# Attention with a bias on one core: transposes of later pairs issued into a PSUM buffer's gap, evacuations queued ahead of newer products

## The chip, the cores and the metric

One Trainium2 chip, of which the kernel uses one core. The metric is device time in microseconds; the number compared is the median of several executions. Beside it stands one profiled execution, from which all rows below come.

## The reference

Four batches of eight heads, 1024 positions, head dimension 64, and one bias matrix that all heads share:

```python
def reference(q, k, v, bias):            # q, k, v: [4, 8, 1024, 64]; bias: [1, 1, 1024, 1024]
    scale = 1.0 / np.sqrt(head_dim)
    scores = scale * np.matmul(q, k.transpose(0, 1, 3, 2))
    scores = scores + bias
    scores_max = np.max(scores, axis=-1, keepdims=True)
    attn = np.exp(scores - scores_max) / (np.sum(np.exp(scores - scores_max), axis=-1, keepdims=True) + 1e-8)
    return np.matmul(attn, v).astype(np.float32)
```

## The kernel before

The kernel uses exp(s + bias) = exp(s) * exp(bias): `eb` holds exp(bias) transposed, made once, and every tile of exp(scores) is multiplied by it. A column of ones in `vall` gives the row sums with the last product, so the division is done on the small output.

The 32 heads are worked in 16 pairs. A pair's K and Q are loaded (`load_qk`, GpSimd's queue, three buffers), transposed on TensorE into the PSUM tile `px` (16 transposes for K, 16 for Q) and copied out by VectorE into `kT` and `qT` (the latter times `mask`, so that each head meets only its own rows).

The unit of work is a block of 128 keys by 512 queries of one head: 512 blocks, 32 for a pair, named `banks` in the code. They run through a chain of four engines' steps:

- TensorE: three blocks of scores (`s_slot`, a "slot", into one of two PSUM buffers `ps` of three banks).
- ScalarE: one exp over the whole slot, 128x1536, into `E` (twelve buffers of two slots).
- VectorE: `mul_pair`, the product with `eb`, two blocks at a time.
- TensorE again: `av_bank` (below: AV), four matmuls of a block's `E` against `vall`, summed over eight key chunks in the PSUM tile `po`. After the eighth, VectorE evacuates `po`: a reciprocal `rs` and a multiplication into `oall` (below: the evacuation). Two query halves make an output, which SyncE's queue writes.

[...] The other two are the buffers named `xa` and `xb`: `po` of a pair's head 0 uses `xa`, of head 1 `xb`, and `px` uses the same two, Q's in `xa`, K's in `xb`. So a transpose must wait until the sum that was in its buffer is evacuated, and the next sum must wait until the transpose is copied out.

The order of everything is written out by hand under `tc.manual_schedule()`: each engine gets its instructions in the order in which the loop over `order` issues them. One step of the loop issues a slot of scores (or one of six pieces of the bias, early on), then up to three products, then three or four blocks of AV (`quota`), and behind a block of AV with `kc == 7` its evacuation. AV takes the eight blocks of head 0 first, then those of head 1 (`av_order`). The list `pend_t` says at which count of AV blocks a later pair is transposed; its check stands inside the AV loop:

```python
while t_next < len(pend_t) and pend_t[t_next][2] <= av_next and av_next % 8 == 0:
    pr, which, _ = pend_t[t_next]
    transpose(pr, which)
```

The count is a multiple of eight, so a transpose is issued right behind the block that completed a sum, and behind that sum's evacuation on VectorE. Pairs 2 to 15 are transposed in this way, 28 transposes of 16 matmuls; pairs 0 and 1 are transposed in the first steps.

Of the kernel before, what the change touches and what calls it, by code (L numbers as in the profile page):

```python
# [9 lines left out]
BF = mybir.dt.bfloat16  # L10
ACTF = mybir.ActivationFunctionType
ALU = mybir.AluOpType
# [3 lines left out]
def kernel(  # L16
# [15 lines left out]
    nc = tc.nc  # L32
    B, H, S, D = q.shape
    P = 128
    NCH = S // P
    D1 = D + 1
    NP = B * H // 2
# [12 lines left out]
    kvp = ctx.enter_context(tc.tile_pool(name="kvp", bufs=3))  # L50
    ep = ctx.enter_context(tc.tile_pool(name="ep", bufs=12))
    op = ctx.enter_context(tc.tile_pool(name="op", bufs=2))
    small = ctx.enter_context(tc.tile_pool(name="small", bufs=4))
    ps_s = ctx.enter_context(tc.tile_pool(name="ps_s", bufs=2, space=bass.MemoryType.PSUM))
    ps_x = ctx.enter_context(tc.tile_pool(name="ps_x", bufs=1, space=bass.MemoryType.PSUM))
# [5 lines left out]
    mask = consts.tile([P, 2, S], BF)  # L61
# [3 lines left out]
    trs = {}  # L65

    def load_qk(pr):
        qr = raw.tile([P, 2, NCH, D], BF, name="qr")
        kr = raw.tile([P, 2, NCH, D], BF, name="kr")
        nc.gpsimd.dma_start(out=kr.rearrange("p t c d -> p t (c d)"), in_=kf[pr])  # L70
        nc.gpsimd.dma_start(out=qr.rearrange("p t c d -> p t (c d)"), in_=qf[pr])  # L71
        raws[pr] = (qr, kr)

    def load_v(pr):
        for t in range(2):
            nc.gpsimd.dma_start(out=vall[:, 2 * pr + t, :, :D], in_=vf[pr, :, t])  # L76

    def transpose(pr, which):
        src = raws[pr][which]
        px = ps_x.tile([P, NCH, P], BF, tag="xa" if which == 0 else "xb", name="px")  # L80
        for c in range(NCH):
            for t in range(2):
                nc.tensor.transpose(px[t * D:(t + 1) * D, c, :], src[:, t, c, :], ident[:])  # L83
        if which == 0:

            dst = kvp.tile([P, 2, NCH * P], BF, name="qT")
            nc.vector.tensor_tensor(dst[:], px.rearrange("p c q -> p (c q)").unsqueeze(1).to_broadcast([P, 2, NCH * P]),  # L87
                                    mask[:], op=ALU.mult)
        else:
            dst = kvp.tile([P, NCH, P], BF, name="kT")  # L90
            nc.vector.tensor_copy(dst[:], px[:])  # L91
        trs[(pr, which)] = dst


    banks = [(pr, h, qh, kc) for pr in range(NP) for qh in range(2) for kc in range(NCH) for h in range(2)]
    NB = len(banks)
# [4 lines left out]
    def s_slot(g):  # L101
        ps = ps_s.tile([P, 3, HQ], F32, tag="s", name="ps")
        sl = slots[g]
        for j, (pr, h, qh, kc) in enumerate(sl):
            qT, kT = trs[(pr, 0)], trs[(pr, 1)]
            nc.tensor.matmul(ps[:, j, :], kT[:, kc, :], qT[:, h, qh * HQ:(qh + 1) * HQ],  # L106
                             start=True, stop=True)
        if g % 2 == 0:
            etiles[g // 2] = ep.tile([P, 6, HQ], BF, name="E")
        e = etiles[g // 2]  # L110
        o = 3 * (g % 2)
        n = len(sl)
        nc.scalar.activation(e[:, o:o + n, :], ps[:, :n, :], ACTF.Exp, scale=scale)  # L113

    def b_slot(qh, kcs):
        ps = ps_s.tile([P, 3, 2 * HQ], BF, tag="s", name="pb")
        for j, kc in enumerate(kcs):
            for i in range(QC):
                nc.tensor.transpose(ps[:, j, i * P:(i + 1) * P],  # L119
                                    btraw[:, qh * QC + i, :].rearrange("p (kp kc) -> p kc kp", kc=NCH)[:, kc, :],  # L120
                                    ident[:])
        n = len(kcs)
        nc.scalar.activation(eb[:, qh, kcs[0]:kcs[0] + n, :], ps[:, :n, :HQ], ACTF.Exp)  # L123

    def mul_pair(b):
        pr, h, qh, kc = banks[b]
        e = etiles[b // 6]
        o = b % 6
        nc.vector.tensor_tensor(e[:, o:o + 2, :], e[:, o:o + 2, :],  # L129
                                eb[:, qh, kc, :].unsqueeze(1).to_broadcast([P, 2, HQ]),  # L130
                                op=ALU.mult)
# [4 lines left out]
    def av_bank(b):  # L136
        pr, h, qh, kc = banks[b]
        if kc == 0:
            po[h] = ps_x.tile([P, QC, D1], F32, tag="xa" if h == 0 else "xb", name="po")
        acc = po[h]  # L140
        e = etiles[b // 6]
        for i in range(QC):
            nc.tensor.matmul(acc[:, i, :], e[:, b % 6, i * P:(i + 1) * P], vall[:, 2 * pr + h, kc, :],  # L143
                             start=(kc == 0 and i == 0), stop=(kc == NCH - 1), skip_group_check=True)
        if kc == NCH - 1:
            if qh == 0:
                oalls[h] = op.tile([P, NCH, D], F32, tag=f"o{h}", name="oall")
            oall = oalls[h]
            rs = small.tile([P, QC, 1], F32, name="rs")
            nc.vector.reciprocal(rs[:], acc[:, :, D:D1])  # L150
            nc.vector.tensor_tensor(oall[:, qh * QC:(qh + 1) * QC, :], acc[:, :, :D],  # L151
                                    rs[:].to_broadcast([P, QC, D]), op=ALU.mult)
            if qh == 1:
                nc.sync.dma_start(out=of[2 * pr + h], in_=oall[:])


    av_order = []
# [3 lines left out]
    with tc.manual_schedule():  # L161

        nc.vector.memset(warm[:], 0.0)
        nc.scalar.activation(warm[:], warm[:], ACTF.Exp)  # L164
        make_identity(nc, ident[:])
        load_qk(0)
        nc.gpsimd.dma_start(out=btraw[:, :QC, :], in_=bf_[:, :QC, :])
        nc.vector.memset(vall[:, :, :, D:D1], 1.0)
        for t in range(2):
            for u in range(2):  # L170
                nc.vector.memset(mask[t * D:(t + 1) * D, u, :], 1.0 if t == u else 0.0)  # L171
        load_v(0)
        load_qk(1)
        nc.gpsimd.dma_start(out=btraw[:, QC:, :], in_=bf_[:, QC:, :])
        load_v(1)
        load_qk(2)
        transpose(0, 1)
        transpose(0, 0)

        order = [("S", g) for g in range(NS)]  # L180
        halves = [(0, 1, 2), (3, 4, 5), (6, 7)]
        for at, x in ((3, (0, halves[0])), (5, (0, halves[1])), (7, (0, halves[2])),
                      (9, (1, halves[0])), (11, (1, halves[1])), (13, (1, halves[2]))):
            order.insert(at, ("B",) + x)

        done_b = -1
        mul_next = 0
        eb_have = set()
        av_next = 0
        muls_at = {}  # L190
        pend_t = [(1, 1, 4), (1, 0, 5)]
        for pr in range(2, NP):
            pend_t += [(pr, 0, (pr - 2) * 32 + 8), (pr, 1, (pr - 2) * 32 + 16)]
        t_next = 0
        loaded = 2
        for step, item in enumerate(order):
            if item[0] == "S":
                g = item[1]
                s_slot(g)
                exp_b = min(NB, 3 * (g + 1))  # L200
            else:
                b_slot(item[1], item[2])
                for kc in item[2]:
                    eb_have.add((item[1], kc))
                exp_b = done_b + 1

            n = 0
            while mul_next + 2 <= exp_b and n < 3:
                pr, h, qh, kc = banks[mul_next]
                if (qh, kc) not in eb_have:  # L210
                    break
                mul_pair(mul_next)
                muls_at[mul_next] = muls_at[mul_next + 1] = step
                mul_next += 2
                n += 1
            done_b = exp_b - 1

            quota = 4 if (exp_b - av_next) > 18 else 3
            while quota and av_next < NB:
                b = av_order[av_next]  # L220
                if muls_at.get(b, 10 ** 9) > step - 2:
                    break

                av_bank(b)
                av_next += 1
                quota -= 1
                while t_next < len(pend_t) and pend_t[t_next][2] <= av_next and av_next % 8 == 0:
                    pr, which, _ = pend_t[t_next]
                    transpose(pr, which)
                    t_next += 1  # L230
                    if which == 1:
                        if pr + 1 < NP:
                            load_qk(pr + 1)
                        if pr < NP:
                            load_v(pr)
            if step == 3:
                for _ in range(2):
                    pr, which, _ = pend_t[t_next]
                    transpose(pr, which)
                    t_next += 1  # L240

        while mul_next < NB:
            mul_pair(mul_next)
            mul_next += 2
        while av_next < NB:
            av_bank(av_order[av_next])
            av_next += 1


# [28 lines left out]
```

## Time and profile before

| what | value |
|---|---|
| median of 3 runs | 390.25 us (389.04 to 392.25) |
| profiled execution | 391.52 us, its span 389.5 us |
| mean granted TensorE clock | 0.858 |
| ScalarE, TensorE, VectorE busy | 244.1, 266.8, 234.3 us |
| HBM read, written | 29.36, 8.39 MB |

The span runs from the first to the last instruction on the core; the execution's time is 2.0 us longer. Busy times are unions of an engine's instructions. Matmuls are pipelined and their ends modelled, so TensorE's busy time is more than its work.

### The profile page before, as it was taken

Reading aid. Unit: us, or ns where it says so; the run is one execution under the profiler, and the core shown is the slowest. Engines: PE = TensorE matmul, PEld = TensorE weight load, DVE = VectorE, ACT = ScalarE, POOL = GpSimd, SP = SyncE. Lnnn points to the kernel's source line nnn. Section 1 sums busy time; section 2 is a strip of 40 time slices with the busy share of each in tenths; the row PEclk is TensorE's granted clock in tenths of the full one; section 3 lists DMA queues with packets and bytes.
Section 4 is the critical chain, followed back from the end, with each engine's and each line's share of the span. In section 5 each row is a group of like instructions: output and inputs, shape, how many; then the busy total and the mean of one; then the engine's idle time right before and its main releaser. Section 6 shows DMA issues by size and latency. Waiting matters only on the chain. (4 is left out here: it accounts for less than half of the span.)

```text
span 389.5 us, 7214 instructions
## 1 busy us (share of the span) xinstructions
PE 266.8 (69%) x3136; PEld 165.9 (43%) x3136; DVE 234.3 (60%) x422; ACT 244.1 (63%) x179; POOL 52.6 (14%) x72
## 2 busy tenths in 40 slices
PE   2756866758566697665966669476776756759894
PEld 1435434435343454433544345243443534435553
DVE  5353475865638566374566856557485473855885
ACT  1682865946558485482756749456594554947992
POOL 8340301103030030300303012030220000000000
PEclk9996799988879786697789969889696897988997
DMA  7998710808026080360803508071190010100111
GB/s 119 202 184 90 81 56 6 130 2 108 29 40 97 2 108 28 48 89 3 107 29 55 83 0 121 16 80 58 23 141 0 3 56 0 44 12 13 44 56 55
DMA packets 46911, 23.53 MB, mean 60 GB/s; under 512 B 34336, under 2 KB 42528, under 8 KB 46624
## 3 DMA queue, kind: packets, MB, share of 16 engines
q0 software_dynamic: 42272, 14.68, 34.0%
q1 hardware_dynamic: 4608, 8.39, 5.8%
q8 instruction: 24, 0.39, 0.4%
q14 instruction: 7, 0.06, 0.0%
HBM read 29.36 MB, written 8.39 MB: 97 GB/s over the span
## 5 line engine op out<-in xcount | busy, mean ns | idle before, releaser
L113 ACT ACTIVATE E<-ps 128x1536 bf16<-128x1536 f32 x171 | 235.4, 1476 | 129.1 <-PE ps L106 90.0
L129 DVE TENSOR_TENSOR E<-E,eb 128x1024 bf16<-128x1024 bf16 x256 | 169.2, 689 | 113.7 <-ACT E L113 101.5
L106 PE MATMUL ps<-qT,kT 128*128 128x512 bf16 x512 | 164.4, 437 | 17.1 <-ACT E L113 15.1
L143 PEld LDWEIGHTS <-E 128*128 128x128 bf16 x2048 | 99.6, 106 | 63.6 <-issue 22.7
L143 PE MATMUL po<-vall,E 128*128 128x65 bf16 x2048 | 110.0, 206 | 6.7 <-DVE E L129 5.1
L106 PEld LDWEIGHTS <-kT 128*128 128x128 bf16 x512 | 49.5, 108 | 56.6 <-issue 41.1
L83 PE MATMUL px<-ident,kr 128*64 128x128 bf16 x256 | 15.5, 292 | 50.2 <-DVE oall L151 44.0
L83 PE MATMUL px<-ident,qr 128*64 128x128 bf16 x256 | 13.4, 263 | 44.5 <-DVE oall L151 43.2
L70 POOL DMA_DIRECT2D kr<-in_k_dram x16 | 11.3, 708 | 226.1 <-PE px L83 219.9
L83 PEld LDWEIGHTS <-kr 128*64 128x64 bf16 x256 | 12.3, 153 | 51.7 <-issue 45.3
L83 PEld LDWEIGHTS <-qr 128*64 128x64 bf16 x256 | 10.6, 136 | 46.3 <-issue 44.5
L87 DVE TENSOR_TENSOR qT<-px,mask 128x2048 bf16<-128x2048 bf16 x16 | 19.6, 1224 | 15.4 <-PE px L83 15.4
L76 POOL DMA_DIRECT2D vall<-in_v_dram x32 | 28.1, 885 | 4.3 <-DMA btraw<-in_bias_dram 4.0
L151 DVE TENSOR_TENSOR oall<-po,rs 128x256 f32<-128x256 f32 x64 | 27.2, 424 | 2.2
L91 DVE COPY kT<-px 128x1024 bf16<-128x1024 bf16 x16 | 11.1, 691 | 17.5 <-PE px L83 17.5
L123 ACT ACTIVATE eb<-pb 128x1536 bf16<-128x1536 bf16 (+1 forms) x6 | 7.9, 1309 | 8.5 <-PE pb L119 8.5
L150 DVE RECIPROCAL rs<-po 128x4 f32<-128x4 f32 x64 | 11.3, 176 | 1.4 <-PE po L143 1.4
L71 POOL DMA_DIRECT2D qr<-in_q_dram x16 | 11.7, 728 | 0.8 <-issue 0.4
L119 PE MATMUL pb<-ident,btraw 128*128 128x128 bf16 x64 | 5.9, 252 | 0.5 <-ACT E L113 0.5
L119 PEld LDWEIGHTS <-btraw 128*128 128x128 bf16 x64 | 5.4, 151 | 1.7 <-issue 0.9
L171 DVE MEMSET mask<- 64x1024 bf16 (+1 forms) x4 | 2.8, 698 | 0.5 <-issue 0.2
L164 ACT ACT_TABLE_LOAD x1 | 1.3, 1283 | 0.7 <-PEq L262 0.7
(11 smaller groups left out, 2.6 us busy)
## 6 DMA issues: line engine op xcount, KB each, us to landing
out_dram<-oall SPq DMA_DIRECT2D x32, 256.0 KB, 2.0
kr<-in_k_dram POOLq DMA_DIRECT2D x16, 256.0 KB, 4.0
qr<-in_q_dram POOLq DMA_DIRECT2D x16, 256.0 KB, 5.4
vall<-in_v_dram POOLq DMA_DIRECT2D x32, 128.0 KB, 5.8
btraw<-in_bias_dram POOLq DMA_DIRECT2D x2, 1024.0 KB, 12.3
```

What stands on the lines that cost most here:

```text
L70: nc.gpsimd.dma_start(out=kr.rearrange("p t c d -> p t (c d)"), in_=kf[pr])
L71: nc.gpsimd.dma_start(out=qr.rearrange("p t c d -> p t (c d)"), in_=qf[pr])
L76: nc.gpsimd.dma_start(out=vall[:, 2 * pr + t, :, :D], in_=vf[pr, :, t])
L83: nc.tensor.transpose(px[t * D:(t + 1) * D, c, :], src[:, t, c, :], ident[:])
L87: nc.vector.tensor_tensor(dst[:], px.rearrange("p c q -> p (c q)").unsqueeze(1).to_broadcast([P, 2, NCH * P]), mask[:], op=ALU.mult)
L106: nc.tensor.matmul(ps[:, j, :], kT[:, kc, :], qT[:, h, qh * HQ:(qh + 1) * HQ], start=True, stop=True)
L113: nc.scalar.activation(e[:, o:o + n, :], ps[:, :n, :], ACTF.Exp, scale=scale)
L119: nc.tensor.transpose(ps[:, j, i * P:(i + 1) * P], btraw[:, qh * QC + i, :].rearrange("p (kp kc) -> p kc kp", kc=NCH)[:, kc, :], ident[:])
L129: nc.vector.tensor_tensor(e[:, o:o + 2, :], e[:, o:o + 2, :], eb[:, qh, kc, :].unsqueeze(1).to_broadcast([P, 2, HQ]), op=ALU.mult)
L143: nc.tensor.matmul(acc[:, i, :], e[:, b % 6, i * P:(i + 1) * P], vall[:, 2 * pr + h, kc, :], start=(kc == 0 and i == 0), stop=(kc == NCH - ...
L150: nc.vector.reciprocal(rs[:], acc[:, :, D:D1])
L151: nc.vector.tensor_tensor(oall[:, qh * QC:(qh + 1) * QC, :], acc[:, :, :D], rs[:].to_broadcast([P, QC, D]), op=ALU.mult)
```

## The change

The transposes and the evacuations are split from their second halves. `transpose_pe` issues the 16 matmuls and returns a function that issues VectorE's copy; `av_bank` returns a function that issues the evacuation. A step now issues, in this order: its slot of scores; a waiting transpose's matmuls, if one is due; blocks of AV; one product; the evacuations and copies that are due (`late`); up to two more products. A transpose falls due two steps behind the step in which AV reached its count (`t_wait = step + 2`), and that step issues one block of AV only (`quota = 1`). All later transposes use `xa`, and the counts are such (8 and 24 of a pair's 32) that it is head 0's sum that has just ended, so that head 1's eight blocks run in `xb` meanwhile. The products of a step are those of the slot before (`exp_b = new_b` stands at the end of the step), and a block of AV is issued three steps behind its product (`LAG`) where it was two. K and Q are asked for two pairs ahead instead of one.

```diff
--- before.py
+++ after.py
@@ -76,20 +76,27 @@
             nc.gpsimd.dma_start(out=vall[:, 2 * pr + t, :, :D], in_=vf[pr, :, t])
 
     def transpose(pr, which):
+        transpose_pe(pr, which)()
+
+    def transpose_pe(pr, which):
         src = raws[pr][which]
-        px = ps_x.tile([P, NCH, P], BF, tag="xa" if which == 0 else "xb", name="px")
+        px = ps_x.tile([P, NCH, P], BF, tag="xb" if pr < 2 and which else "xa", name="px")
         for c in range(NCH):
             for t in range(2):
                 nc.tensor.transpose(px[t * D:(t + 1) * D, c, :], src[:, t, c, :], ident[:])
-        if which == 0:
-
-            dst = kvp.tile([P, 2, NCH * P], BF, name="qT")
-            nc.vector.tensor_tensor(dst[:], px.rearrange("p c q -> p (c q)").unsqueeze(1).to_broadcast([P, 2, NCH * P]),
-                                    mask[:], op=ALU.mult)
-        else:
-            dst = kvp.tile([P, NCH, P], BF, name="kT")
-            nc.vector.tensor_copy(dst[:], px[:])
-        trs[(pr, which)] = dst
+
+        def copy():
+            if which == 0:
+
+                dst = kvp.tile([P, 2, NCH * P], BF, name="qT")
+                nc.vector.tensor_tensor(
+                    dst[:], px.rearrange("p c q -> p (c q)").unsqueeze(1).to_broadcast([P, 2, NCH * P]),
+                    mask[:], op=ALU.mult)
+            else:
+                dst = kvp.tile([P, NCH, P], BF, name="kT")
+                nc.vector.tensor_copy(dst[:], px[:])
+            trs[(pr, which)] = dst
+        return copy
 
 
     banks = [(pr, h, qh, kc) for pr in range(NP) for qh in range(2) for kc in range(NCH) for h in range(2)]
@@ -142,7 +149,10 @@
         for i in range(QC):
             nc.tensor.matmul(acc[:, i, :], e[:, b % 6, i * P:(i + 1) * P], vall[:, 2 * pr + h, kc, :],
                              start=(kc == 0 and i == 0), stop=(kc == NCH - 1), skip_group_check=True)
-        if kc == NCH - 1:
+        if kc < NCH - 1:
+            return None
+
+        def evac():
             if qh == 0:
                 oalls[h] = op.tile([P, NCH, D], F32, tag=f"o{h}", name="oall")
             oall = oalls[h]
@@ -152,6 +162,7 @@
                                     rs[:].to_broadcast([P, QC, D]), op=ALU.mult)
             if qh == 1:
                 nc.sync.dma_start(out=of[2 * pr + h], in_=oall[:])
+        return evac
 
 
     av_order = []
@@ -183,67 +194,83 @@
                       (9, (1, halves[0])), (11, (1, halves[1])), (13, (1, halves[2]))):
             order.insert(at, ("B",) + x)
 
-        done_b = -1
+        mul_done = {}
+        eb_have = set()
         mul_next = 0
-        eb_have = set()
+        exp_b = 0
         av_next = 0
-        muls_at = {}
-        pend_t = [(1, 1, 4), (1, 0, 5)]
+
+        pend_t = []
         for pr in range(2, NP):
-            pend_t += [(pr, 0, (pr - 2) * 32 + 8), (pr, 1, (pr - 2) * 32 + 16)]
-        t_next = 0
-        loaded = 2
-        for step, item in enumerate(order):
-            if item[0] == "S":
-                g = item[1]
-                s_slot(g)
-                exp_b = min(NB, 3 * (g + 1))
-            else:
-                b_slot(item[1], item[2])
-                for kc in item[2]:
-                    eb_have.add((item[1], kc))
-                exp_b = done_b + 1
-
-            n = 0
-            while mul_next + 2 <= exp_b and n < 3:
+            pend_t += [(pr, 0, (pr - 2) * 32 + 8), (pr, 1, (pr - 2) * 32 + 24)]
+        gap = None
+        LAG = 3
+
+        def muls(n):
+            nonlocal mul_next
+            while n and mul_next + 2 <= exp_b:
                 pr, h, qh, kc = banks[mul_next]
                 if (qh, kc) not in eb_have:
                     break
                 mul_pair(mul_next)
-                muls_at[mul_next] = muls_at[mul_next + 1] = step
+                mul_done[mul_next] = mul_done[mul_next + 1] = step
                 mul_next += 2
-                n += 1
-            done_b = exp_b - 1
-
+                n -= 1
+
+        t_wait = None
+        for step, item in enumerate(order):
+            prev_b = exp_b
+            if item[0] == "S":
+                g = item[1]
+                s_slot(g)
+                new_b = min(NB, 3 * (g + 1))
+            else:
+                b_slot(item[1], item[2])
+                new_b = exp_b
+            late = []
+            if step == 3:
+                transpose(1, 1)
+                transpose(1, 0)
+                load_qk(3)
             quota = 4 if (exp_b - av_next) > 18 else 3
+            if t_wait is not None and step >= t_wait:
+                pr, which, _ = pend_t.pop(0)
+                late.append(transpose_pe(pr, which))
+                t_wait = None
+                quota = 1
+                if which == 1:
+                    if pr + 2 < NP:
+                        load_qk(pr + 2)
+                    load_v(pr)
             while quota and av_next < NB:
                 b = av_order[av_next]
-                if muls_at.get(b, 10 ** 9) > step - 2:
+                if mul_done.get(b, 10 ** 9) > step - LAG:
                     break
-
-                av_bank(b)
+                e = av_bank(b)
+                if e:
+                    late.append(e)
                 av_next += 1
                 quota -= 1
-                while t_next < len(pend_t) and pend_t[t_next][2] <= av_next and av_next % 8 == 0:
-                    pr, which, _ = pend_t[t_next]
-                    transpose(pr, which)
-                    t_next += 1
-                    if which == 1:
-                        if pr + 1 < NP:
-                            load_qk(pr + 1)
-                        if pr < NP:
-                            load_v(pr)
-            if step == 3:
-                for _ in range(2):
-                    pr, which, _ = pend_t[t_next]
-                    transpose(pr, which)
-                    t_next += 1
-
-        while mul_next < NB:
-            mul_pair(mul_next)
-            mul_next += 2
+                if pend_t and av_next == pend_t[0][2]:
+                    t_wait = step + 2
+
+            muls(1)
+            for f in late:
+                f()
+            muls(2)
+            exp_b = new_b
+            if item[0] == "B":
+                for kc in item[2]:
+                    eb_have.add((item[1], kc))
+
         while av_next < NB:
-            av_bank(av_order[av_next])
+            muls(1)
+            b = av_order[av_next]
+            while mul_next <= b:
+                muls(1)
+            e = av_bank(b)
+            if e:
+                e()
             av_next += 1
 
 
```

On VectorE, around the transposes of pair 7 in the kernel before (`qT` and `kT` are the copies of a transpose; L150 and L151 are an evacuation, L129 a product):

```order
L129 TENSOR_TENSOR E_1677<-E_1677,eb_82 128x1024
L150 RECIPROCAL rs_1689<-po_1641 128x4
L151 TENSOR_TENSOR oall_1688<-po_1641,rs_1689 128x256
L87 TENSOR_TENSOR qT_1709<-px_1692,mask_83 128x2048
L129 TENSOR_TENSOR E_1677<-E_1677,eb_82 128x1024 x2
L129 TENSOR_TENSOR E_1739<-E_1739,eb_82 128x1024 x3
L150 RECIPROCAL rs_1766<-po_1711 128x4
L151 TENSOR_TENSOR oall_1765<-po_1711,rs_1766 128x256
L91 COPY kT_1786<-px_1769 128x1024
```

Each copy stands directly behind an evacuation, with no product between them, and the evacuation behind products of the slot just issued.

The same place in the changed kernel (L136 is the product, L160 and L161 the evacuation):

```order
L160 RECIPROCAL rs_1718<-po_1656 128x4
L161 TENSOR_TENSOR oall_1717<-po_1656,rs_1718 128x256
L136 TENSOR_TENSOR E_1654<-E_1654,eb_82 128x1024
L136 TENSOR_TENSOR E_1697<-E_1697,eb_82 128x1024 x2
L92 TENSOR_TENSOR qT_1768<-px_1746,mask_83 128x2048
L136 TENSOR_TENSOR E_1697<-E_1697,eb_82 128x1024
L136 TENSOR_TENSOR E_1744<-E_1744,eb_82 128x1024
L160 RECIPROCAL rs_1795<-po_1703 128x4
L161 TENSOR_TENSOR oall_1794<-po_1703,rs_1795 128x256
L136 TENSOR_TENSOR E_1744<-E_1744,eb_82 128x1024 x2
```

Three products now stand between the evacuation that frees the buffer and the copy, and one product of the copy's own step stands ahead of it.

On TensorE, the start of pair 7's K transpose in the kernel before, with the engines that a row waits for:

```order
L143 LDWEIGHTS E_1638
L143 MATMUL po_1711<-vall_84,E_1638 128x65
L83 LDWEIGHTS kr_1520 [waits DVE_49,DMASW4_49]
L83 MATMUL px_1769<-ident_79,kr_1520 64x128 [waits PE_49]
L83 LDWEIGHTS kr_1520
```

And in the changed kernel, where the sum whose buffer it takes is `po_1780`; the last block of that sum, and the start of the transpose:

```order
L150 MATMUL po_1780<-vall_84,E_1697 128x65
L150 LDWEIGHTS E_1591 [waits DVE_49]
L150 MATMUL po_1831<-vall_84,E_1591 128x65 [waits PE_49]
...
L113 MATMUL ps_1865<-qT_1495,kT_1644 128x512 [waits Activation_49]
L113 LDWEIGHTS kT_1644
...
L86 LDWEIGHTS kr_1361 [waits DVE_49,DMASW2_49]
L86 MATMUL px_1870<-ident_79,kr_1361 64x128 [waits PE_49]
```

Before, the wait for VectorE stands right behind the last AV matmul of the sum `po_1711` that must be evacuated; now two slots of scores and five blocks of AV into `po_1831` lie between.

## Rows read from the trace of the kernel before

**Rows 1.** The page's head: span, and busy time, share and instructions of each engine.

```profile
span 389.5 us, 7214 instructions
...
PE 266.8 (69%) x3136; PEld 165.9 (43%) x3136; DVE 234.3 (60%) x422; ACT 244.1 (63%) x179; POOL 52.6 (14%) x72
```

**Rows 2.** Waits over the span: who waited for whom, total us, times, longest.

```profile
POOL kr L70 <- PE px L83: 219.9, 11, 24.5
...
PE px L83 <- DVE oall L151: 87.2, 28, 3.6
...
PE po L143 <- DVE E L129: 5.1, 16, 0.8
```

**Rows 3.** Costliest groups on the page: busy us, mean ns | idle before, releaser.

```profile
L113 ACT ACTIVATE E<-ps 128x1536 bf16<-128x1536 f32 x171 | 235.4, 1476 | 129.1 <-PE ps L106 90.0
L129 DVE TENSOR_TENSOR E<-E,eb 128x1024 bf16<-128x1024 bf16 x256 | 169.2, 689 | 113.7 <-ACT E L113 101.5
...
L87 DVE TENSOR_TENSOR qT<-px,mask 128x2048 bf16<-128x2048 bf16 x16 | 19.6, 1224 | 15.4 <-PE px L83 15.4
...
L151 DVE TENSOR_TENSOR oall<-po,rs 128x256 f32<-128x256 f32 x64 | 27.2, 424 | 2.2
L91 DVE COPY kT<-px 128x1024 bf16<-128x1024 bf16 x16 | 11.1, 691 | 17.5 <-PE px L83 17.5
L123 ACT ACTIVATE eb<-pb 128x1536 bf16<-128x1536 bf16 (+1 forms) x6 | 7.9, 1309 | 8.5 <-PE pb L119 8.5
L150 DVE RECIPROCAL rs<-po 128x4 f32<-128x4 f32 x64 | 11.3, 176 | 1.4 <-PE po L143 1.4
```

**Rows 4.** Timeline around pair 7's K transpose: start us, us, engine, line, idle before.

```profile
155.30 0.99 PE L106 MATMUL ps<-qT,kT 128*128 128x512 bf16 x3
...
157.81 1.29 DVE L129 TENSOR_TENSOR E<-E,eb 128x1024 bf16<-128x1024 bf16 x2 [0.72 <-ACT E L113]
159.02 0.17 DVE L150 RECIPROCAL rs<-po 128x4 f32<-128x4 f32 x1
159.23 0.42 DVE L151 TENSOR_TENSOR oall<-po,rs 128x256 f32<-128x256 f32 x1
...
159.79 1.06 PE L83 MATMUL px<-ident,kr 128*64 128x128 bf16 x16 [3.39 <-DVE oall L151]
...
161.22 1.47 PE L106 MATMUL ps<-qT,kT 128*128 128x512 bf16 x3
...
162.78 1.45 ACT L113 ACTIVATE E<-ps 128x1536 bf16<-128x1536 f32 x1 [5.01 <-PE ps L106]
...
163.16 1.47 PE L106 MATMUL ps<-qT,kT 128*128 128x512 bf16 x3
```

**Rows 5.** Timeline of the same kernel where no transpose is near.

```profile
166.39 8.16 ACT L113 ACTIVATE E<-ps 128x1536 bf16<-128x1536 f32 x6 [0.27 <-PE ps L106]
...
166.51 0.81 PE L106 MATMUL ps<-qT,kT 128*128 128x512 bf16 x3
...
167.16 0.53 PE L143 MATMUL po<-vall,E 128*128 128x65 bf16 x12
...
167.89 0.81 PE L106 MATMUL ps<-qT,kT 128*128 128x512 bf16 x3 [0.21 <-ACT E L113]
```

**Rows 6.** Timeline of the start, pair 1's Q transpose and the first steady exp.

```profile
16.88 0.64 PE L83 MATMUL px<-ident,qr 128*64 128x128 bf16 x16 [0.64 <-DMA qr<-in_q_dram]
...
18.31 1.45 ACT L113 ACTIVATE E<-ps 128x1536 bf16<-128x1536 f32 x1 [1.92 <-PE ps L106]
...
31.06 1.47 PE L119 MATMUL pb<-ident,btraw 128*128 128x128 bf16 x12
```

**Rows 7.** Timeline, ScalarE's last exps.

```profile
353.11 29.26 ACT L113 ACTIVATE E<-ps 128x1536 bf16<-128x1536 f32 x22 [4.14 <-PE ps L106]
```

**Rows 8.** Stretches with and without transposes: us, PE, PEld, DVE, ACT, POOL busy; clock, DMA, GB/s.

```profile
150.00:166.00 16.00, 12.40 (x114) 7.66 (x115) 6.47 (x11) 7.09 (x5) 3.16 (x4) 0.61 0.25 33
...
355.00:381.00 26.00, 23.00 (x296) 13.83 (x295) 22.37 (x44) 26.00 (x20) 0.00 (x0) 1.00 0.11 42
```

## The prediction

> **What bounds the kernel now.** I read the page's head first, then the waits, then a stretch of the timeline that holds one transpose, then one that holds none. No engine is near full: ScalarE is busy 244.1 us of 389.5, VectorE 234.3, and TensorE's 266.8 is a modelled figure [rows 1]. So the time is made by engines waiting for one another in turn. The costliest exp group shows the sum of it: ScalarE sat idle 129.1 us, mostly for scores that TensorE had not made [rows 3]. The waits show why TensorE was late: 28 times a transpose (`px`) waited for an evacuation (`oall`), 87.2 us in all [rows 2]. 28 is the number of transposes of pairs 2 to 15.
>
> One of them in full [rows 4]: the scores of a slot start at 155.30. Their exp must end before VectorE makes the two products that were issued ahead of the evacuation (157.81); only then come the reciprocal (159.02) and the multiplication (159.23), and the transpose starts at 159.79, after TensorE has stood 3.39 us. Behind it in TensorE's order stand the next scores, at 161.22, so ScalarE starts at 162.78 after 5.01 us of idleness. From scores to scores that is 5.92 us. And TensorE comes back slowly: the next slot takes 1.94 us (161.22 to 163.16). [...]
>
> Without a transpose near, the kernel runs at ScalarE's pace. Six exps take 8.16 us, the first 1.45, the others 1.342 apart; TensorE's scores take 0.65 us, its three blocks of AV the rest, and it then stands 0.21 us for ScalarE [rows 5], so its work is 1.17 us of a slot of 1.34. From 355 to 381 ScalarE was busy all of 26.00 us at a granted clock of 1.00 [rows 8].
>
> **The floor that the change could reach.** ScalarE's first exp behind the start-up is at 18.31 [rows 6]; the wait ahead of it is for loads, which the change doesn't move. From there 168 slots at 1.342 are 225.5 us, and the five remaining exps of the bias are 6.4 (7.9 less the first at about 1.5) [rows 3]. The last exp ended at 382.37 and the span at 389.5 [rows 1, 7], a tail of 7.1 which stays: its last product and its last sum are in the same order. 18.3 + 225.5 + 6.4 + 7.1 = 257.3 us of span. So the 28 transposes cost (389.5 - 257.3) / 28 = 4.7 us each now. What is left of that in the changed kernel is the question.
>
> **The change part by part.**
>
> *Products one slot behind.* An evacuation no longer stands behind products that wait for the exp of the same step's slot. It waits for one product at most, and that one's exp belongs to the slot before, which is through when TensorE starts the new scores, since `ps` has two buffers. This takes the exp and a product out of the chain in [rows 4]. It costs no instruction.
>
> *Transposes two steps later.* TensorE does two slots of scores and up to seven blocks of AV between the end of a sum and the transpose into its buffer. The evacuation is queued one product (0.66 us, 169.2 over 256) behind its slot's exp and takes 0.60 (0.42 + 0.18) [rows 3]; the transpose comes about 2.1 us (1.34 + the 0.65 of the scores, and their wait) after that exp. The 3.39 us go, with some 0.8 to spare if VectorE is on time.
>
> *The transpose's own time on TensorE.* 16 matmuls took 0.64 us in an undisturbed place [rows 6] and 1.06 behind a long wait [rows 4]. I take 0.64, as nothing waits ahead of it now. The step that holds it issues one block of AV (0.17, a third of the 0.52 from 167.16 to where the wait of 0.21 began [rows 5]): 0.65 + 0.64 + 0.17 = 1.46 against 1.34, so the next scores come 0.1 late, less than TensorE's reserve. Cost 0; at 1.06 it would be 0.2 each.
>
> *The copy out, the new wait.* In the next step AV comes back to head 0, whose sum needs `xa`, and must wait for the copy. Behind that wait are queued the rest of the step's AV and then the scores that ScalarE wants. Count from the moment when the exp ahead of the copy's step ends. One product, 0.66 with its start; then `qT`, 1.22 [rows 3]: 1.9 us. Then two to four blocks of AV, 0.5, and the scores with their way to ScalarE, 0.85: 3.25. ScalarE wants them after two slots, 2.69. So it loses 0.6 us at a Q transpose if VectorE is on time. `kT` takes 0.69: 2.7 us, no loss. VectorE is not quite on time: its work per slot is (169.2 + 27.2 + 19.6 + 11.3 + 11.1) / 171 = 1.39 us [rows 3] against 1.34, though neighbouring instructions overlap a little (two products in 1.29 [rows 4]). A copy that is late by one product costs 0.6 more. I take 0.2 of lateness for Q and 0.3 for K, so 0.8 and 0.3. Bounds: nothing at all, and 1.5 for each of the 28, which is two products and an evacuation late. Each idle also starts an exp anew, 1.45 in place of 1.342, 0.1.
>
> *AV three steps behind its product.* This takes away waits that total 5.1 us on TensorE before AV [rows 2]; they were beside ScalarE's pace, so I count 0, and 5 at most as a gain. The twelve `E` buffers hold 72 blocks, and a backlog of some 24 fits.
>
> *Loads.* The issues move on GpSimd's queue: V of a pair now stands behind K and Q of two pairs on. GpSimd's 219.9 us of waits [rows 2] are for raw buffers, three of them as before; a K load waits for the transpose of the pair three earlier, as before, and V is asked for two pairs before AV needs it. 0.
>
> *Sum.* 14 x (0.8 + 0.3) + 28 x 0.1 = 18.2 us. 257.3 + 18.2 = 275.5 of span. The profiled execution lies 2.0 above its span and the median 1.3 below the profiled execution: 276.2, so **276 us**, with its bounds 257.3 + 0.7 = 258 and 257.3 + 0.7 + 28 x 1.5 = 300.
>
> [...] In the rows the granted clock is 1.00 where TensorE stops for some 0.2 us in each slot, and 0.61 around waits of 3 us [rows 8]. With the long waits gone I expect 1.00 nearly throughout. [...]
>
> **Rivals.**
>
> *VectorE is late at every copy.* The wait for an evacuation is exchanged for one for the copy, with VectorE behind by two products and an evacuation: 1.5 us at each transpose, 300 us. For it: VectorE's 1.39 us a slot, more than ScalarE's. Against: each loss of ScalarE lets VectorE catch up, and by its sum alone (238.4 from 18.8, when pair 1's copies are out, and 3 us for the last output) VectorE would be through at 260.
>
> *The wait stays where it was.* Should VectorE be two slots behind, the transpose would wait for the evacuation as now, for up to 3.1 us (87.2 / 28), but without the exp in the chain. Half of the old cost of 4.7 would be 28 x 2.35 = 66 us on the floor: 324 us. Against it: nothing holds VectorE back by so much, since its products wait only for exps that are through.
>
> [...]
>
> **How the numbers follow.** The forecast (258 to 290) gets 0.75, VectorE late at every copy (290 to 310) 0.15, the wait that stays (310 to 386) 0.06, the low clock, slower than 394, 0.02, something under 258 or within 1% of before 0.02. Eight in ten are held by 261 to 295: from nearly no loss at the copies to 1.3 us at each. A measurement of this kernel can tell about 1% from no change. Faster by more than that: 0.96; within it 0.02; slower 0.02.
>
> **What would show it.** In the changed profile, the transposes' wait for `oall` should fall from 87.2 us to under 10, and AV's wait for `qT` or `kT` should appear, some 0.6 to 1 us at a time, more at Q's than at K's. ScalarE's idle time ahead of its exps should fall from 129.1 us to under 35, its gaps one for a transpose and under 1.5 us. The granted clock should be above 0.95. VectorE should be busy 83% or more. I am wrong if the gaps of ScalarE come at other places than the transposes, if the clock falls below 0.9, or if the products (not the copies) make AV wait.

## The result

| kernel | median, us | ratio to the kernel before, 95% interval |
|---|---|---|
| before | 390.63 (4 runs, 389.04 to 392.25) | |
| changed | 266.75 (4 runs, 266.52 to 266.89) | 0.6828 [0.6799, 0.6857] |

The forecast was 276 us, in a range of 261 to 295. The profiled execution took 266.52 us, with a span of 264.5.

The page of the changed kernel, its head [rows 1] and three groups, the first two the same as in [rows 3], the third TensorE's AV:

```profile
span 264.5 us, 7204 instructions
...
PE 221.0 (84%) x3136; PEld 137.6 (52%) x3136; DVE 227.2 (86%) x422; ACT 240.7 (91%) x179; POOL 52.5 (20%) x72
...
L120 ACT ACTIVATE E<-ps 128x1536 bf16<-128x1536 f32 x171 | 232.4, 1475 | 16.7 <-PE ps L113 14.6
L136 DVE TENSOR_TENSOR E<-E,eb 128x1024 bf16<-128x1024 bf16 x256 | 167.1, 687 | 18.9 <-ACT E L120 14.1
...
L150 PE MATMUL po<-vall,E 128*128 128x65 bf16 x2048 | 94.1, 194 | 16.1 <-DVE qT L92 10.9
```

ScalarE does the same work (240.7 us against 244.1), and its idle time ahead of its exps fell from 129.1 us to 16.7. Its waits, against [rows 2]:

```profile
ACT E L120 <- PE ps L113: 14.6, 11, 9.4
...
PE po L150 <- DVE qT L92: 10.9, 14, 1.0
...
PE po L150 <- DVE kT L97: 4.3, 14, 0.4
```

No transpose waits for `oall` any more; that line of 87.2 us is gone. In its place stand the waits that the change had to bring: AV waits for a copy, 14 times for Q's (0.78 us each) and 14 times for K's (0.31). Where they reach ScalarE is seen in its timeline, which merges exps that follow one another without a gap:

```profile
18.52 1.45 ACT L120 ACTIVATE E<-ps 128x1536 bf16<-128x1536 f32 x1 [1.32 <-PE ps L113]
...
112.34 14.88 ACT L120 ACTIVATE E<-ps 128x1536 bf16<-128x1536 f32 x11 [0.48 <-ACT E L120]
127.78 13.60 ACT L120 ACTIVATE E<-ps 128x1536 bf16<-128x1536 f32 x10 [0.56 <-PE ps L113]
141.70 15.01 ACT L120 ACTIVATE E<-ps 128x1536 bf16<-128x1536 f32 x11 [0.32 <-PE ps L113]
...
231.41 26.68 ACT L120 ACTIVATE E<-ps 128x1536 bf16<-128x1536 f32 x20 [0.32 <-PE ps L113]
```

In the steady part there are 13 gaps, one per pair, of 0.32, 0.48 and 0.56 us in turn (as in the three rows from 112.34 on), 5.8 us in all. The one ahead of 127.78 in full, from the same kernel's timeline:

```profile
122.70 0.42 DVE L161 TENSOR_TENSOR oall<-po,rs 128x256 f32<-128x256 f32 x1
...
123.22 2.04 DVE L136 TENSOR_TENSOR E<-E,eb 128x1024 bf16<-128x1024 bf16 x3
123.24 0.81 PE L113 MATMUL ps<-qT,kT 128*128 128x512 bf16 x3
...
123.98 0.64 PE L86 MATMUL px<-ident,qr 128*64 128x128 bf16 x16
...
124.68 0.81 PE L113 MATMUL ps<-qT,kT 128*128 128x512 bf16 x3
...
125.17 1.22 DVE L92 TENSOR_TENSOR qT<-px,mask 128x2048 bf16<-128x2048 bf16 x1
...
126.45 0.65 PE L150 MATMUL po<-vall,E 128*128 128x65 bf16 x16 [0.95 <-DVE qT L92]
...
126.93 0.81 PE L113 MATMUL ps<-qT,kT 128*128 128x512 bf16 x3
...
127.58 0.53 PE L150 MATMUL po<-vall,E 128*128 128x65 bf16 x12
...
127.95 0.81 PE L113 MATMUL ps<-qT,kT 128*128 128x512 bf16 x3
```

The evacuation that frees the buffer ends at 123.12, and the transposes start at 123.98 without a wait. Their copy stands behind a product, the AV of head 0 behind the copy, and the scores that ScalarE wants behind AV. It is a Q transpose. No K transpose has a gap behind it.

### The profile page after: what moved, and what is told of

The parts are those of the page before. It is cut to its first block, busy times and chain, and to the rows that moved or that the text cites. A ratio compares the mean times of both kernels' runs of the same rounds, so it can differ in the third digit from the quotient of the medians.

```text
span 264.5 us, 7204 instructions
## 1 busy us (share of the span) xinstructions
PE 221.0 (84%) x3136; PEld 137.6 (52%) x3136; DVE 227.2 (86%) x422; ACT 240.7 (91%) x179; POOL 52.5 (20%) x72
## 4 chain that ended last, share of the span: by engine, by line
ACT 44%; DVE 26%; PE 18%; DMA 4%; issue 4%; POOL 2%; ACTq 0%; POOLq 0%
ACT E L120 42%; DVE E L136 16%; PE ps L113 13%; DVE qT L92 5%; PE po L150 5%; DMA qr<-in_q_dram 4%; DVE kT L97 3%; ACT eb L130 2%; DVE oall L161 2%; DVE rs L160 1%; POOL vall L76 1%; POOL kr L70 1%; ACTq L120 0%; POOL qr L71 0%; PE px L86 0%
## 5 line engine op out<-in xcount | busy, mean ns | idle before, releaser
L120 ACT ACTIVATE E<-ps 128x1536 bf16<-128x1536 f32 x171 | 232.4, 1475 | 16.7 <-PE ps L113 14.6
L136 DVE TENSOR_TENSOR E<-E,eb 128x1024 bf16<-128x1024 bf16 x256 | 167.1, 687 | 18.9 <-ACT E L120 14.1
L113 PE MATMUL ps<-qT,kT 128*128 128x512 bf16 x512 | 139.7, 382 | 14.5 <-ACT E L120 10.9
L150 PEld LDWEIGHTS <-E 128*128 128x128 bf16 x2048 | 84.2, 98 | 54.6 <-issue 19.5
L150 PE MATMUL po<-vall,E 128*128 128x65 bf16 x2048 | 94.1, 194 | 16.1 <-DVE qT L92 10.9
L113 PEld LDWEIGHTS <-kT 128*128 128x128 bf16 x512 | 44.2, 98 | 45.1 <-issue 20.7
L161 DVE TENSOR_TENSOR oall<-po,rs 128x256 f32<-128x256 f32 x64 | 27.2, 425 | 2.2
L86 PE MATMUL px<-ident,kr 128*64 128x128 bf16 x256 | 10.6, 228 | 5.8 <-DMA kr<-in_k_dram 5.8
L86 PEld LDWEIGHTS <-kr 128*64 128x64 bf16 x256 | 8.0, 113 | 11.8 <-issue 5.9
L86 PE MATMUL px<-ident,qr 128*64 128x128 bf16 x256 | 10.6, 228 | 2.0 <-DMA qr<-in_q_dram 2.0
L86 PEld LDWEIGHTS <-qr 128*64 128x64 bf16 x256 | 8.0, 113 | 8.3 <-DMA qr<-in_q_dram 5.4
L160 DVE RECIPROCAL rs<-po 128x4 f32<-128x4 f32 x64 | 11.2, 175 | 1.0 <-PE po L150 1.0
```

## The experiments

All but one start from the changed kernel; the lines that differ are shown or told, with `...` where some are left out. The theory: a transpose cost 4.7 us because an exp, products and an evacuation stood in a chain in which TensorE could do nothing else; the order on VectorE and the delay each take a part of that chain out, and what is left is the copy of Q. The rivals: the delay alone does it; or it was the low clock.

**The low clock's share.** The kernel before, with TensorE at work in its waits (26 of the 28), by matmuls whose results the next scores overwrite:

```diff
+    def fill(pr):
+        ps = ps_s.tile([P, 3, HQ], F32, tag="s", name="ps")
+        qT, kT = trs[(pr, 0)], trs[(pr, 1)]
+        for j in range(12):
+            nc.tensor.matmul(ps[:, j % 3, :], kT[:, j % NCH, :], qT[:, 0, :HQ], start=True, stop=True)
+        ready.append(ps)
...
-        ps = ps_s.tile([P, 3, HQ], F32, tag="s", name="ps")
+        ps = ready.pop() if ready else ps_s.tile([P, 3, HQ], F32, tag="s", name="ps")
...
+                    if step > 15 and order[step + 1][0] == "S":
+                        fill(slots[order[step][1]][0][0])
                     transpose(pr, which)
```

> The kernel before, with TensorE kept at work in 26 of its 28 waits: ahead of a transpose it makes 12 score matmuls into the buffer of the next slot (0.216 us each, 2.6 us in a wait of 3.1), which that slot's own scores then overwrite; they do no part of the result, and all else is the kernel before. Theory (about 2 us of the 4.7 that a transpose cost are the low clock behind the wait: 0.4 on the transposes, 0.6 on each of three slots): 26 x 2.0 = 52 us less, about 338 (325 to 350), with a granted clock above 0.97. Rival (the cost is the wait itself, and the slow slots behind it are hidden): 380 to 392 us.

It took 361.13 us, beside 389.73 for the kernel before in the same runs, a ratio of 0.9263 [0.9210, 0.9317]. The mean granted clock was 0.977, and one transpose in its timeline reads:

```profile
147.14 2.75 PE L107 MATMUL ps<-qT,kT 128*128 128x512 bf16 x12 [0.41 <-ACT E L122]
...
150.46 0.64 PE L83 MATMUL px<-ident,kr 128*64 128x128 bf16 x16 [0.57 <-DVE oall L160]
...
152.18 10.85 ACT L122 ACTIVATE E<-ps 128x1536 bf16<-128x1536 f32 x8 [3.75 <-issue]
```

28.6 us over 26 waits is 1.1 us each, not 2.0. Neither side's number held: the low clock is a real part of the old cost, but the smaller one. The 1.1 may be a little too low, since only 19 of the 28 transposes still waited for `oall`; the others came when the added matmuls had ended, which may have held them up. With a granted clock of 1.00 (145 to 165 us) ScalarE still lost 3.75 us at a transpose (5.01 in [rows 4]).

**The order on VectorE alone.** No delay: evacuation, transpose and copy are issued in the step that ends the sum.

```diff
-                    t_wait = step + 2
+                    pr, which, _ = pend_t.pop(0)
+                    muls(1)
+                    for f in late:
+                        f()
+                    late = []
+                    transpose(pr, which)
...
```

> No delay at all: in the step that ends a sum, one product, the evacuation, the transpose and its copy are issued at once, then the rest of AV; products stay one slot behind and AV three steps. Theory: the exp is out of the chain, but TensorE still stands about 1.5 us for each evacuation, its next scores come 1.9 us late, and ScalarE loses 1.7 us at each of 28 transposes: about 305 us (295 to 315), with a granted clock near 1.00, since no wait is near 3 us. So some 85 us of the gain would come from the order on VectorE and some 40 from the delay. Rival 1 (the order on VectorE is nothing, the delay all): 370 to 390 us. Rival 2 (the low clock made most of the old loss, and it is gone as soon as the waits are halved): 270 to 280 us.

318.06 us. The waits:

```profile
PE px L86 <- DVE oall L161: 47.9, 28, 1.8
```

28 waits of 1.71 us on average, a little more than the 1.5 expected. Two neighbouring transposes, the first of K, the second of Q, and the stretch around the second (us, then busy time of PE, PEld, DVE, ACT, POOL, then granted clock):

```profile
154.84 0.64 PE L86 MATMUL px<-ident,kr 128*64 128x128 bf16 x16 [1.78 <-DVE oall L161]
...
156.63 6.82 ACT L120 ACTIVATE E<-ps 128x1536 bf16<-128x1536 f32 x5 [1.87 <-PE ps L113]
...
163.53 0.70 PE L86 MATMUL px<-ident,qr 128*64 128x128 bf16 x16 [1.66 <-DVE oall L161]
...
166.16 1.45 ACT L120 ACTIVATE E<-ps 128x1536 bf16<-128x1536 f32 x1 [2.71 <-issue]
```

```profile
163.00:169.00 6.00, 5.25 (x68) 3.49 (x70) 4.02 (x7) 3.10 (x3) 0.00 (x0) 0.72 0.08 23
```

Around the first the granted clock was 1.00 (150 to 163), and ScalarE lost 1.87 us. Around the second it was 0.72 in the six microseconds around the end of the wait, and ScalarE lost 2.90 us (2.71 and, one exp later, 0.19). The page has the clock at 0.7 or 0.8 in five of its 40 slices ahead of the tail, one of them at the second transpose. If each of the five is one transpose like it, which is an estimate, they make some 5 of the 13 us above the 305 that were expected; the rest is 1.9 where 1.7 was taken, and an exp started anew each time. Rival 1 fell (without the delay, the order with all else that the change brings is worth 72 us), and rival 2 with it.

**The delay alone.** Products of the slot just issued, all else as changed: `exp_b = new_b` and the bias pieces' entry in `eb_have` move from the end of the step to ahead of its products. The evacuation still stands behind one product of its step only, where the kernel before issued up to three ahead of it.

> The products of a step are again those of the slot just issued, so every evacuation and copy stands behind a product that waits for that slot's exp; the two steps of delay, the buffers and AV's three steps are the changed kernel's. Theory: an evacuation is through 1.34 us later, which the two steps just fail to hide (0.5 us of wait), and a copy too, which nothing hides: ScalarE loses about 2.0 us at each Q and 1.5 at each K transpose, 50 us in place of 7; about 308 us (298 to 315). Rival (the two steps of delay hide it alone): 267 to 272 us.

304.86 us, ratio 0.7803 [0.7758, 0.7849]. One Q transpose:

```profile
122.14 0.64 PE L86 MATMUL px<-ident,qr 128*64 128x128 bf16 x16 [0.56 <-DVE oall L161]
...
123.44 0.69 DVE L136 TENSOR_TENSOR E<-E,eb 128x1024 bf16<-128x1024 bf16 x1 [0.24 <-ACT E L120]
...
124.05 1.22 DVE L92 TENSOR_TENSOR qT<-px,mask 128x2048 bf16<-128x2048 bf16 x1
...
125.32 0.53 PE L150 MATMUL po<-vall,E 128*128 128x65 bf16 x12 [1.54 <-DVE qT L92]
...
126.53 5.48 ACT L120 ACTIVATE E<-ps 128x1536 bf16<-128x1536 f32 x4 [1.34 <-PE ps L113]
```

Both waits that were expected are there, 0.56 us for the evacuation and 1.54 for the copy, whose product has just waited for its exp. The rival, 267 to 272, fell.

**One step of delay instead of two.** `t_wait = step + 1`.

> The transposes are issued one step behind the end of their sum instead of two; the rest is the changed kernel's. Theory (an evacuation queued behind one finished product is through about 1.3 us after its slot's exp, so a second step of delay is worth only what is left of that): TensorE waits some 0.55 us for each evacuation and ScalarE loses 0.43 at each of 28 transposes, 12 us in place of 7, while the waits for the copies go, since the buffer has a step more; about 272 us (268 to 274), against 266.75 for two steps. Rival (the delay is what carries the gain, half of the old 3.1 us wait for each step): 290 to 310 us.

269.69 us. Transposes waited 25 times for `oall`, 0.56 us each, and the waits for the copies were gone, as expected.

```profile
PE px L86 <- DVE oall L161: 14.1, 25, 0.6
```

The second step of delay is worth 2.9 us.

**The place within the step.** Products ahead of evacuations and copies: `muls(3)` in place of `muls(1)`, and no `muls(2)`.

> The changed kernel with the step's evacuations and copies behind all of its products; the products are still those of the slot before. In 9 of the 28 steps of a transpose there is a second product, so 4 Q and 5 K copies come 0.6 us later. Theory: 4 x 0.6 + 5 x 0.3 = 4 us, 267 to 272, about 270. Rival (the place within the step counts at every evacuation): 280 us or more.

272.05 us, just above the range. ScalarE's gaps tell which steps it was:

```profile
115.14 14.88 ACT L120 ACTIVATE E<-ps 128x1536 bf16<-128x1536 f32 x11 [1.09 <-issue]
130.59 6.82 ACT L120 ACTIVATE E<-ps 128x1536 bf16<-128x1536 f32 x5 [0.56 <-PE ps L113]
137.97 6.82 ACT L120 ACTIVATE E<-ps 128x1536 bf16<-128x1536 f32 x5 [0.56 <-ACT E L120]
145.10 15.01 ACT L120 ACTIVATE E<-ps 128x1536 bf16<-128x1536 f32 x11 [0.32 <-PE ps L113]
```

Where the changed kernel had 0.48 there is now 1.09, one product more, the gaps of 0.56 and 0.32 are the same, and the gap ahead of 137.97 is new: the K transpose with a second product, 0.56 instead of the 0.3 that I took.

**The copy first.** In the step of a transpose its copy goes ahead of the first product.

```diff
+            first = None
...
-                late.append(transpose_pe(pr, which))
+                first = transpose_pe(pr, which)
...
+            if first:
+                first()
             muls(1)
```

> In the step of a transpose its copy is queued ahead of the step's first product instead of behind it; nothing else moves. Theory (all that is left to win in the steady part is ScalarE's 0.44 us at each Q transpose, lost because AV waits 0.8 us for the copy of 1.22 us that stands behind a product of 0.6): the wait falls to about 0.2 us and the loss to none, 5.8 us of idle time and 13 slow starts of 0.1: about 260 us (259 to 262). Rival (the loss comes from TensorE's own 0.64 us of transposes in the step, or the product that is now later is missed by AV): 266 us or more.

259.55 us, ratio 0.6648 [0.6602, 0.6695]. The waits for `qT` are 14 of 0.31 us, and ScalarE runs without a gap to the end:

```profile
PE po L150 <- DVE qT L92: 4.3, 14, 0.4
```

```profile
31.26 219.72 ACT L120 ACTIVATE E<-ps 128x1536 bf16<-128x1536 f32 x163
```

**The copy of Q twice.** The same instruction again behind itself, for pairs 2 to 15.

> The changed kernel with the copy of Q made twice at each of 14 transposes, 1.14 us more on VectorE ahead of the release of the buffer. Theory (AV waits for the copy, and ScalarE loses what the wait is over its reserve, 0.44 us now): each of 14 loses 1.14 more, 16 us, about 283 (279 to 288). Rival (ScalarE's loss there is from the transposes on TensorE, and VectorE's time hides): 266 to 270 us.

295.89 us, above the range: 29.1 us over 14 copies is 2.1 each, where 1.14 was expected. AV's waits for `qT` grew from 0.78 to 2.04 us, 1.26 each, so the sign and the place are the theory's. Most of the rest goes with the clock: at four of the 14 the page's slice (7.4 us) has it at 0.9 or more, and ScalarE lost 1.2 to 1.8 us; at ten the slice has 0.7 or 0.8, and ScalarE lost 2.3 to 3.0. The first row below is one of the four, the two behind it one of the ten, and below them is the stretch behind its wait, at 0.50 (columns as above):

```profile
175.86 14.88 ACT L124 ACTIVATE E<-ps 128x1536 bf16<-128x1536 f32 x11 [1.76 <-issue]
```

```profile
139.79 1.06 PE L154 MATMUL po<-vall,E 128*128 128x65 bf16 x16 [2.21 <-DVE qT L96]
...
142.17 3.03 ACT L124 ACTIVATE E<-ps 128x1536 bf16<-128x1536 f32 x2 [2.87 <-PE ps L117]
```

```profile
140.00:143.00 3.00, 2.78 (x31) 1.91 (x30) 2.09 (x4) 0.83 (x1) 0.00 (x0) 0.50 0.00 0
```

**AV two steps behind instead of three.** `LAG = 2`.

> The changed kernel with AV two steps behind its product instead of three. Theory (the third step only shortens waits that lay beside ScalarE's pace): the same within 1%, 265 to 269 us. Rival (with VectorE busy 86% its products are late, and AV waits for them): 272 us or more.

262.67 us: neither. It is 4 us faster than with three. The waits for `qT` fell to 10, of 6.7 us in all, those for `kT` to 5, of 0.9 in all.

```profile
PE po L150 <- DVE qT L92: 6.7, 10, 0.8
```

The order shows a reason: between a Q transpose and the next sum in its buffer there stand 1 to 3 blocks of head 1 with three steps, and 3 to 5 with two, in which the copy is made. If that is the reason, the gain is the same wait as that of the copy first, and the two don't add:

> The copy ahead of the step's first product, as in the run that took 259.55 us, and AV two steps behind its product, as in the one that took 262.67. Theory (both take away the same wait for the copy of Q, and what is left is ScalarE's own pace): no more than either, 259 to 260.5 us. Rival (the two gains, 7 and 4 us, have different causes and add): 255 to 256 us.

258.52 us (257.80 to 259.74), ratio 0.6620 [0.6595, 0.6646]: half a microsecond under the expected range, and well above the 255 to 256 of the rival. They don't add.

**The start.** The copy first, and pair 1's transposes one step later (`if step == 4`).

> The copy ahead of the first product, and pair 1's transposes in the start-up issued behind the fourth slot of scores instead of ahead of it (one step later), so that those scores no longer wait for pair 1's loads. Theory (ScalarE is the bound from its first exp on, and its idle 1.8 us ahead of the fourth slot is the only gap that is left): 1.0 to 1.8 us less than 259.55, about 258 us. Rival (the loads that are asked for later, or VectorE's copies that come later, give it back in the start-up): 259 to 261 us.

258.78 us (258.66 to 258.92), ratio 0.6621 [0.6600, 0.6642]: 0.8 us less than the copy first alone, which is under what two sets of runs tell apart. In the profile ScalarE's gap of 1.8 us ahead of the fourth exp is gone and gaps of 1.05 and 0.37 ahead of pieces of the bias have come, so the steady run of 163 exps starts at 30.61 instead of 31.26.

## Why the prediction was right, and which term was off

**What bound the kernel before** held: 28 waits, and no engine full. By the run with TensorE at work in its waits, the 4.7 us of a transpose split into about 1.1 for the low clock and 3.6 for the chain. The prediction had put no number on the clock's share; the 2.0 expected for that run summed TensorE's slow slots as if all of that time reached ScalarE.

**The floor of 257.3 us** held. The changed kernel's 264.5 less its 13 gaps (5.8) and 13 slow starts of 0.1 is 257.4; with the copy first the span is 257.4. It is ScalarE, whose 163 exps then fill 219.72 us. That it comes out to 0.1 us is luck, since pieces that are off by up to 1 us cancel: the exps take 1.348 us each in place of 1.342, the tail was 6.4 us in place of 7.1, the first steady exp at 18.52 in place of 18.31. Nor is it a hard bound: it takes the wait for loads at the start as given, and with pair 1's transposes later the span is 256.7.

**Products one slot behind and the transposes' delay** did what the prediction gave them, with the 0.8 us to spare (123.12 to 123.98): the wait for `oall` went from 87.2 us to none. One without the other, the order takes the kernel to 318.06 us and the delay to 304.86, gains of 72 and 85 where both give 124. They overlap, since either shortens the same long waits and with them the low clock behind them (on average 0.969 and 0.991, against 0.858 before); how much of the overlap is which was not measured. Both runs keep what else the change has, the buffer `xa` for all later transposes, the loads two pairs ahead and AV's three steps; of these, only the last was tried by itself.

**The transposes' own time** was 0.64 us as taken, and from scores to scores their step took 1.44 us (123.24 to 124.68) where the prediction had 1.46. It cost ScalarE nothing: with the copy first, the same transposes leave no gap.

**The new wait for the copy** is the step that was mis-sized, 18.2 us where 7.2 were lost. The arithmetic of a copy on time was right: 0.6 at Q, and 0.56 measured where AV needs the buffer soonest (0.48 and 0.32 elsewhere, where fewer blocks of AV stand between the copy and the scores), none at K. Taking 0.6 at all 14 was 2.6 us too much, and 28 exps started anew where there were 13 another 1.5. Wrong above all was the lateness that I added, 0.2 and 0.3, 7.0 us in all. It came from summing VectorE's busy time to 1.39 us a slot against ScalarE's 1.34. That sum counts the stretch in which two neighbours overlap twice: three products took 2.04 us at 123.22, and the copy behind them started 1.95 us after the first of them did. The same five groups add up to 236.0 us in the changed kernel's page, while VectorE was busy in 227.2 us in all, which is 1.33 a slot. It still stood 18.9 us ahead of products, 14.1 of them for exps. It was on time. One of the signs that the prediction named came otherwise for the same reason: the gaps are one for each Q transpose only, and AV's waits for K's copies are 0.31 us. Some of the miss doesn't show in the time: the prediction set the median 0.7 us above the span, and it lies 2.2 above.

**AV three steps behind** was costed at nothing, with 5 us at most as a gain. It is a loss of 4 us, through the copy's wait and not through AV's (with the copy first, two steps or three differ by 1.0 us, within the noise): this was in the order, and I had looked only for waits on products.

**The rivals.** VectorE late at every copy, the wait that stays, and the low clock did not come. The one that is made on purpose, the copy of Q twice, shows that the first, large enough, brings the last with it: with waits of about 2 us the clock fell at ten of 14. One price was misread: two products and an evacuation are 1.9 us (2 x 0.66 + 0.60), not 1.5, which puts the upper bound of 300 too low. No run shows the low clock in every slot. The trace of the kernel before has a slot of 1.94 us (161.22 to 163.16) and K's 16 transposes in 1.06 (159.79 to 160.85) [rows 4], both at a granted clock of 0.50; an estimate with these for all 168 slots and 28 transposes, from the first steady scores at 17.5 on, is 17.5 + 326 + 29.7 + 7.1 + 0.7 = 381 us, which is faster than the kernel before and not slower than 394.

**The clock** was 1.00 from 100 to 160, a stretch with eight groups of 16 transposes (their busy time on PE and PEld, then the granted clock):

```profile
100.00:160.00 60.00, 5.10 (x128) 3.81 (x128) 1.00 0.64 89
```

Each group took 0.64 us amid other matmuls. With 5.1 us of transposes in 60, the rest of the stream being other matmuls, the granted clock did not fall, as the prediction expected; a larger share of transposes was not tried.

## What to carry to other kernels

Where an in-order engine serves both a stream and a hand-over that another engine waits for, queue the hand-over ahead of the stream's newest work, and put other work between the end of a sum and whatever reuses its buffer. Then look at the next reuse in the same way: here the copy out became the wait, and one line that put it first gave 7 us more. When an engine looks too busy by its summed durations, compare starts with starts before calling it late.

## What the runs showed of the hardware

The granted clock fell behind single waits that were shorter than the 3 us of the kernel before: to 0.50 behind one of 2.21 us (140 to 143 us) and 0.58 behind one of 2.09 (122 to 126), both in the copy of Q twice, and to 0.72 in the six microseconds around the end of one of 1.66 (the order alone). The length of the wait alone doesn't decide it: in the latter run the clock stayed at 1.00 through one of 1.78 (150 to 163 us). In the former the waits for `qT` took 2.04 us on average and 2.2 at most, and at four of the 14 the page has 0.9 or more. In the steady part of the changed kernel, with waits of up to 1.0 us, it was 1.00 (40 to 220 us). Behind such a fall ScalarE lost about 1 us more than where the clock held, 2.9 us against 1.9 in the order alone. What else decides was not tried.

From start to start, a block of AV costs TensorE 0.12 us: four went through in 0.48 us behind a wait (126.45 to the scores at 126.93) and three in 0.37 without one (127.58 to 127.95). The 0.17 a block that the prediction took from [rows 5] runs to the modelled end of the last one.
